# A hybrid encoder layer on one core: attention's products with v taken two steps at a time, sums of the down weights moved to gate/up, Silu, other tile sizes

## The chip, the cores and the metric

The kernel runs on one core of a Trainium2 chip. The core has TensorE (PE, whose weight loads are listed apart as PEld), VectorE (DVE), ScalarE (ACT), GpSimd (POOL) and SyncE (SP, which here only issues DMAs). The metric is the device time of one execution in microseconds (us), as the median of several executions. The kernel before took 1590.09 us as the median of three (1587.43 to 1590.85).

## What is computed

One layer on 1024 frames of 1024 features, in float32:

```python
h = rmsnorm(x, norm_mix_g)
z = h @ w_in
qa, fa, ia, ga, qb, kb, vb, gate_a, gate_b = jnp.split(z, split_at, axis=-1)
oa = hgrn2_mixer(qa, fa, ia, ga, ...)        # a gated recurrence, 4 heads of 128
ob = band_attention(qb, kb, vb, ...)         # 8 heads of 64, each chunk of 64 frames sees itself and 8 before
merged = sigmoid(gate_a) * (oa @ w_branch_a) + sigmoid(gate_b) * (ob @ w_branch_b)
x = x + merged @ w_out
h2 = rmsnorm(x, norm_ffn_g)
x = x + (silu(h2 @ w_ffn_gate) * (h2 @ w_ffn_up)) @ w_ffn_down      # 2816 inner features
h3 = rmsnorm(x, norm_ple_g)
x = x + sigmoid(h3 @ w_ple_gate) * (p @ w_ple_proj)
```

## The kernel before

Each large product keeps float32 accuracy by splitting both operands into a rounded part (`hi`) and a rest (`lo`): ACT copies the raw tile into `hi`, POOL or DVE subtracts to get `lo`, and PE adds three products, hi·hi, hi·lo and lo·hi (`gemm`, L137). Most matmuls have 128 rows, 128 columns of weights and 512 moving columns. Activations lie with features on partitions, so 1024 frames make two halves of 512.

The stages follow each other in `run` (L1861):

- **Recurrence.** `hgrn_in` (L311) makes the inputs of a head and `hgrn_mix` (L387) runs the recurrence of the head before; `weave` interleaves the two. The step `near` (L353) prepares the next head at the end of one.
- **Attention.** `attention` (L638) runs 32 steps, one for each pair of heads and each block of 128 frames. A step holds scores of two heads, transposes of q and k for the next step (`attn_stack`), transposes of the probabilities of the former step (`attn_pt`, inner name `pt`), products with v of the step before that (`attn_pv`, inner name `pv`) and, through `feed`, matmuls of later inputs. `pv(n)` has ten products of 128 x 128 by 64, two heads side by side in the two halves of the array's columns; a float32 product is two instructions. `pts` tiles have four buffers.
- **Gates, branches and the output product** (`gate_units`, `branches`, `out_proj`).
- **Gate/up.** `ff_pairs` (L1548) goes over 21 units after the first, which `second_part` does. An even unit makes 256 columns of the gate product, an odd one the same columns of the up product. `strassen` (L1461) computes a unit with seven products of 12 matmuls in three PSUM banks, where an eighth would be plain. The second product's bank is read into `u2` by DVE before the fourth product adds to it, and again into `u3` before the sixth adds to it. The stream `side` is advanced after each product: it makes the next unit's weights (`strassen_weights`, L1418), loads those of the unit after (`strassen_load`) and, in even units, forms sums of activations (`keep_acts`, L1519). `unit_gate` (L1404) finishes a gate product: DVE multiplies by the norm's row factor `rb`, ACT takes the sigmoid, POOL multiplies the two and then by `rb` once more.
- **Down, and the last product** (`ff_down`, `ple`).

The products of `out_proj`, `ff_down` and `ple` are also Strassen's, over quadrants a11, a21, a22, a12 of the weights; four sums of the quadrants (S1 to S4) are made in the kernel, stored to DRAM and read back as weights later. For `w_out` there are 4 such jobs, for `w_ffn_down` 11, each of four additions on 128 x 512. Before the change, 8 of the 15 jobs run on POOL during the recurrence, in halves of 256 columns (`quad_piece` and `quad_early`, L1083 to L1115, put beside the main stream by `beside`), and the other 7 on POOL in `gate_units` (`quad_slow`, L1047).

DVE, ACT and POOL work strictly in the order of the program where calls go through `self.V`, `self.A` and `self.G` (class `Pinned`), and so do PE and SP's queue. Because these helpers record the operation, most rows of a profile have L54 as their line; matmuls have L83, transposes L86, DMAs L78. In a row, `pm` is a PSUM tile, `s` a 128 x 1024 slot, `t` a 128 x 512 temporary (`stmp`), `q` a sum of weights, `wr` a raw weight, `whi`/`wlo` and `wh`/`wl` its split, `m` a small tile, `d` a DRAM tile. DMAs into SBUF wait until a tile's former content has been used.

Of the kernel before, what the change touches and what calls it, by code (L numbers as in the profile page):

```python
# [10 lines left out]
F32 = mybir.dt.float32  # L11
F32R = mybir.dt.float32r
U8 = mybir.dt.uint8
# [4 lines left out]
P = 128  # L18
# [15 lines left out]
PLAIN = 4  # L34
QUADS = 8

# [20 lines left out]
class Trunk:  # L57
# [175 lines left out]
    def setup(self):  # L233
        nc, d = self.nc, self.d
        cp = self.cp
        self.cols = cp.tile([P, N_COL], F32, name="cols")
        nc.scalar.dma_start(self.cols, d["cols"])
        self.eye = cp.tile([P, P], F32, name="eye")
        self.ones = cp.tile([P, 1], F32, name="ones")
        nc.vector.memset(self.ones, 1.0)  # L240
        self.onesr = cp.tile([P, P], F32R, name="onesr")
# [23 lines left out]
    def first_norm(self):  # L265
# [6 lines left out]
        for k in range(KC):  # L272
# [20 lines left out]
            if k == 3:  # L293
                self.load(self.eye, self.d["eye"])
                self.load(self.masks, self.d["masks"])
            if k:
# [341 lines left out]
    def attention(self):  # L638
# [40 lines left out]
        for n in range(whole + 2):  # L679
# [8 lines left out]
            if n < whole:  # L688
                scores(n, 1)
            drain(st)  # L690
            pt(n - 1, 1)
            next(feed, None)
            stage(n, 0)
            stage(n, 1)
            pv(n - 2)
            pt(n - 1, 0)
# [98 lines left out]
    def gate_units(self, sums):  # L795
# [42 lines left out]
        for n in range(units):  # L838

            def side():  # L840
                more = self.strassen_weights() if n + 1 < units else self.branch_first()
                if n == 0:
                    yield
                    yield
                next(more, None)
                if n + 2 < units:
                    self.strassen_load()
                yield
                for i, _ in enumerate(more):
                    for _ in range(1 + i % 2):  # L850
                        next(sums, None)
                    yield
# [229 lines left out]

    def quad_piece(self, src, k, sums, half):  # L1083

        G, cols = self.nc.gpsimd, HALF // 2
        w = self.slot(late=True)
        at = slice(half * cols, half * cols + cols)
        self.load(w[:, :].rearrange("p (i c) -> p i c", i=4), src.rearrange("p (i c) -> p i c", i=4)[:, :, at])
        for _ in range(5):
            yield  # L1090
        a11, a21, a22, a12 = [w[:, i * cols:i * cols + cols] for i in range(4)]
        for out, x, y, op in ((a22, a21, a22, ALU.add), (a21, a11, a21, ALU.subtract), (a11, a22, a11, ALU.subtract), (a12, a12, a11, ALU.subtract)):
            G.tensor_tensor(out, x, y, op)  # L1093
            yield
        yield
        to = slice(k % 2 * HALF + at.start, k % 2 * HALF + at.stop)
        for kind, part in zip(("S2", "S3", "S1", "S4"), (a11, a21, a22, a12)):
            if k % 2 == 0 and half == 0:
                sums[kind, k // 2] = self.spill()
            self.store(sums[kind, k // 2][:, to], part)  # L1100
        yield
        yield

    def quad_early(self, jobs):

        pieces = [self.quad_piece(*job, half) for job in jobs for half in range(2)]
        live = []
        while pieces or live:
            if pieces:
                live.append(pieces.pop(0))  # L1110
            for _ in range(6):
                for x in list(live):
                    if next(x, x) is x:
                        live.remove(x)
                yield  # L1115
# [288 lines left out]
    def unit_gate(self, c, half, ps):  # L1404
# [143 lines left out]
    def ff_pairs(self):  # L1548
        V, A, G = self.V, self.A, self.G

        units = len(self.sorder)
        self.acts = {}
        self.strassen_load()
        for n in range(1, units):
# [3 lines left out]
            def side():  # L1558
# [182 lines left out]
    def ple(self):  # L1741
# [32 lines left out]
        def after(kind, u, ps):  # L1774
# [35 lines left out]
        def side():  # L1810
# [30 lines left out]
            for i in range(4):  # L1841
                some(4)
                yield
            del todo[:]
# [16 lines left out]
    def run(self):  # L1861
# [18 lines left out]
        with ExitStack() as es:  # L1880
# [12 lines left out]
            with ExitStack() as mixer:  # L1893
                self.masks = mixer.enter_context(tc.tile_pool(name="levels", bufs=1)).tile([P, len(LEVELS), 64], U8, name="masks")
# [3 lines left out]
                jobs = [(d["oq"][k], k, self.osums) for k in range(4)] + [(d["wq"][k], k, self.sums) for k in range(NFF // 2)]  # L1898
                sums = self.quad_early(jobs[:QUADS])
                drain(beside(self.hgrn_in(0, outs), sums))  # L1900
                for h in range(3):
                    weave(beside(self.hgrn_in(h + 1), sums), self.hgrn_mix(h), 41500, 17000)
                self.feed = self.attn_in()
                weave(beside(chain(self.attn_v(), islice(self.feed, FIRST)), sums), self.hgrn_mix(3), 41500 + 1300 * FIRST, 17000)
                drain(sums)
# [52 lines left out]
def beside(main, side):  # L1958
    for x in main:
        next(side, None)  # L1960
        yield x

# [113 lines left out]
```

## Time and profile before

| | |
|---|---|
| median of three runs | 1590.09 us |
| the profiled execution, its own time | 1588.19 us |
| its span, first to last instruction | 1585.9 us |
| PE busy in the span | 1559.4 us |
| DVE busy | 1166.6 us |
| ACT busy | 639.8 us |
| POOL busy | 802.0 us |
| mean granted clock of PE | 0.996 |

The profile is one execution. A row of its timeline gives the start, the length, engine, line, operation, tiles (out<-in), shape and number of the merged instructions, and in brackets how long the engine was idle before and what released it. A row of its groups gives, behind the bar, busy us in all, mean ns of one, and the idle time before. PE's matmuls are pipelined, so two rows may overlap; the distance of their starts is what a matmul costs.

### The profile page before, as it was taken

How to read it: one execution, taken by the hardware profiler on the slowest of the kernel's cores; microseconds unless marked ns; L12 is line 12 of the kernel's file. 1: busy time of each engine (PE TensorE's matmuls, PEld its weight loads, DVE VectorE, ACT ScalarE, POOL GpSimd, SP SyncE). 2: the span in 40 equal slices, each digit the busy share in tenths (PEclk: the TensorE clock that was granted, in tenths of full speed). 3: DMA queues.
4: the chain of work that ended last, by engine and by line, in shares of the span. 5: the costliest groups of instructions: out<-in, count | busy, mean ns of one | idle time of the engine just before them, and what ended most of it. 6: DMA issues, size and time to landing. Idle time of an engine off the chain costs nothing.

```text
span 1585.9 us, 21744 instructions
## 1 busy us (share of the span) xinstructions
PE 1559.4 (98%) x8224; PEld 1311.1 (83%) x8224; DVE 1166.6 (74%) x1670; ACT 639.8 (40%) x1057; POOL 802.0 (51%) x461
## 2 busy tenths in 40 slices
PE   8999999999999999999999999999999999999997
PEld 6898888878888888888888888888888888888886
DVE  5656675468778778644898988888888856765658
ACT  6321211157777643421377322232222234445453
POOL 3764542123113059625330877777777754645454
PEclk9999999999999999999999999999999999999999
DMA  5443220220113358675244433333333278885344
GB/s 189 138 156 119 90 97 27 66 89 27 48 41 107 140 191 306 239 292 212 71 149 172 159 100 100 100 100 113 104 112 107 89 255 321 296 274 196 126 133 158
DMA packets 92649, 230.40 MB, mean 145 GB/s; under 512 B 9856, under 2 KB 26880, under 8 KB 92032
## 3 DMA queue, kind: packets, MB, share of 16 engines
q1 hardware_dynamic: 92400, 229.00, 42.1%
q8 instruction: 64, 1.05, 0.3%
q14 instruction: 41, 0.34, 0.1%
q10 hardware_dynamic: 144, 0.02, 0.0%
HBM read 163.70 MB, written 65.27 MB: 144 GB/s over the span
## 4 chain that ended last, share of the span: by engine, by line
PE 80%; DVE 6%; DMA 6%; POOL 4%; issue 2%; ACT 2%; SPq 1%; POOLq 0%; ACTq 0%; DVEq 0%
PE pm L83 77%; DVE s L54 3%; PE pm L86 3%; POOL wl L126 2%; DMA d<-s 1%; POOL s L1093 1%; DMA s<-in_oq 1%; DMA wr<-d 1%; DVE m L54 1%; SPq L78 1%; DMA wr<-in_qk 1%; DVE q L54 0%; POOL s L54 0%; ACT wh L123 0%; DMA wr<-in_fm 0%
## 5 line engine op out<-in xcount | busy, mean ns | idle before, releaser
L83 PE MATMUL pm<-s,wh 128*128 128x512 f32 (+1 forms) x1712 | 532.1, 392 | 6.6 <-ACT wh L123 5.2
L83 PE MATMUL pm<-s,whi 128*128 128x512 f32 x1568 | 483.0, 389 | 0.6 <-DVE t L54 0.6
L126 POOL TENSOR_TENSOR wl<-wr,wh 128x1024 fp32r<-128x1024 f32 (+2 forms) x108 | 269.5, 2500 | 321.1 <-ACT wh L123 314.9
L83 PEld LDWEIGHTS pm<-s,wh 128*128 128x128 f32 x1712 | 319.9, 189 | 73.5 <-ACT wh L123 5.6
L83 PEld LDWEIGHTS pm<-s,whi 128*128 128x128 f32 x1568 | 294.2, 188 | 61.9 <-DVE t L54 1.0
L83 PE MATMUL pm<-s,wl 128*128 128x512 f32 (+1 forms) x856 | 334.1, 390 | 0.3 <-POOL wl L126 0.3
L54 DVE TENSOR_TENSOR s<-s,s 128x512 f32<-128x512 f32 (+4 forms) x213 | 255.9, 1230 | 92.4 <-ACT s L54 58.3
L83 PE MATMUL pm<-s,wlo 128*128 128x512 f32 x784 | 305.2, 389 | 0.0
L83 PE MATMUL pm<-wh,s 128*128 128x256 f32 (+1 forms) x896 | 239.3, 341 | 0.0
L123 ACT CAST wh<-wr 128x1024 fp32r<-128x1024 f32 (+2 forms) x114 | 114.7, 1007 | 261.7 <-PE pm L83 132.8
L83 PEld LDWEIGHTS pm<-s,wl 128*128 128x128 f32 x856 | 161.3, 188 | 34.8 <-POOL wl L126 1.4
L83 PEld LDWEIGHTS pm<-s,wlo 128*128 128x128 f32 x784 | 147.2, 188 | 31.1 <-DVE wlo L54 0.5
L83 PEld LDWEIGHTS pm<-wh,s 128*128 128x128 f32 x896 | 155.4, 191 | 13.8
L83 PE MATMUL pm<-wl,s 128*128 128x256 f32 (+1 forms) x448 | 148.0, 330 | 0.4 <-POOL wl L126 0.4
L54 DVE TENSOR_TENSOR t<-pm,t 128x512 f32<-128x512 f32 x138 | 94.7, 686 | 71.4 <-PE pm L83 69.3
L54 POOL TENSOR_TENSOR wlo<-wr,whi 128x512 fp32r<-128x512 f32 (+1 forms) x53 | 109.9, 2083 | 72.2 <-ACT whi L54 72.2
L54 DVE TENSOR_TENSOR s<-pm,s 128x512 f32<-128x512 f32 (+1 forms) x134 | 87.3, 680 | 79.9 <-PE pm L83 78.7
L54 ACT CAST whi<-q 128x512 fp32r<-128x512 f32 (+1 forms) x81 | 61.5, 759 | 160.3 <-DVE q L54 140.5
L54 POOL TENSOR_TENSOR s<-s,t 128x512 f32<-128x512 f32 x44 | 76.6, 1741 | 81.7 <-ACT t L54 81.7
L54 ACT CAST s<-s 128x1024 fp32r<-128x1024 f32 (+1 forms) x94 | 90.2, 980 | 68.0 <-DVE s L54 33.7
L54 POOL TENSOR_TENSOR wlo<-q,whi 128x512 fp32r<-128x512 f32 x52 | 89.0, 1712 | 19.0 <-ACT whi L54 19.0
L83 PEld LDWEIGHTS pm<-wl,s 128*128 128x128 f32 x448 | 85.9, 192 | 5.9 <-POOL wl L126 0.6
(146 smaller groups left out, 1953.5 us busy)
## 6 DMA issues: line engine op xcount, KB each, us to landing
s<-d SPq DMA_DIRECT2D x67, 512.0 KB, 6.0
d<-s SPq DMA_DIRECT2D x115, 256.0 KB, 3.3
wr<-d SPq DMA_DIRECT2D x36, 512.0 KB, 3.7
s<-in_wq SPq DMA_DIRECT2D x22, 512.0 KB, 5.6
wr<-in_sg SPq DMA_DIRECT2D x22, 512.0 KB, 4.1
wr<-in_su SPq DMA_DIRECT2D x22, 512.0 KB, 4.1
s<-in_x SPq DMA_DIRECT2D x21, 512.0 KB, 7.8
d<-s SPq DMA_DIRECT2D x18, 512.0 KB, 4.9
```

The lines of the kernel that those rows point to most:

```text
L54: return lambda *a, **k: self.trunk.order(op(*a, **k), self.key)
L78: return self.order(self.nc.sync.dma_start(out, ap), "sp")
L83: return self.order(self.nc.tensor.matmul(*a, **k))
L86: return self.order(self.nc.tensor.transpose(*a, **k))
L123: self.nc.scalar.copy(hi[:, c], raw[:, c])
L126: rest.tensor_tensor(lo[:, c], raw[:, c], f32(hi[:, c]), ALU.subtract)
L1093: G.tensor_tensor(out, x, y, op)
```

## The change

- **Attention.** `pv` is no longer called once in every step between `stage(n, 1)` and `pt(n - 1, 0)`. In odd steps `pv(n - 3)` and `pv(n - 2)` are called one behind the other, after `drain(st)` and ahead of `pt(n - 1, 1)`.
- **Sums of weights.** `quad_early`, `quad_piece` and `beside` go. Five jobs run on POOL in `gate_units`, one addition at each call, and the other ten in `ff_pairs` on DVE, in 20 pieces of 256 columns (`quad_pieces`), which `side` advances from the second unit on. A piece has five steps: load, nothing, two additions, two additions, four stores. They have one buffer of their own (tag `quad`); the temporaries `tmp` fall from eight to seven.
- **Gate function.** ACT takes Silu in place of the sigmoid, and one of POOL's two multiplications goes.
- **Tiles.** `masks` is padded to 8 levels (512 bytes), `onesr` is allocated ahead of `ones`, `state` directly behind `rb`.
- **Down and last product.** The third weight of `ff_down` is asked for after two loads of activations. In `ple`, four additions go from POOL to DVE, and `m_split` is called once more at each of four points.

```diff
             drain(st)
+            if n % 2:
+                pv(n - 3)
+                pv(n - 2)
             pt(n - 1, 1)
             next(feed, None)
             stage(n, 0)
             stage(n, 1)
-            pv(n - 2)
             pt(n - 1, 0)
...
-                for i, _ in enumerate(more):
-                    for _ in range(1 + i % 2):
-                        next(sums, None)
+                for _ in more:
+                    next(sums, None)
                     yield
...
+    def quad_pieces(self, jobs):
+
+        V, cols = self.V, HALF // 2
+        for src, k, sums in jobs:
+            for half in range(2):
+                self.n += 1
+                w = self.fp.tile([P, 4 * cols], F32, tag="quad", name=f"qd{self.n}")
+                at = slice(half * cols, half * cols + cols)
+                self.load(w[:, :].rearrange("p (i c) -> p i c", i=4), src.rearrange("p (i c) -> p i c", i=4)[:, :, at])
+                yield
+                yield
+                a11, a21, a22, a12 = [w[:, i * cols:i * cols + cols] for i in range(4)]
+                V.tensor_tensor(a22, a21, a22, ALU.add)
+                V.tensor_tensor(a21, a11, a21, ALU.subtract)
+                yield
+                V.tensor_tensor(a11, a22, a11, ALU.subtract)
+                V.tensor_tensor(a12, a12, a11, ALU.subtract)
+                yield
+                for kind, part in zip(("S2", "S3", "S1", "S4"), (a11, a21, a22, a12)):
+                    if k % 2 == 0 and half == 0:
+                        sums[kind, k // 2] = self.spill()
+                    self.store(sums[kind, k // 2][:, k % 2 * HALF + at.start:k % 2 * HALF + at.stop], part)
+                yield
...
-        A.activation(s, g[:, hs], AF.Sigmoid)
-        G.tensor_tensor(g[:, hs], g[:, hs], s, ALU.mult)
-        G.tensor_tensor(g[:, hs], g[:, hs], self.rb[:, hs], ALU.mult)
+        A.activation(s, g[:, hs], AF.Silu)
+        G.tensor_tensor(g[:, hs], s, self.rb[:, hs], ALU.mult)
...
+        pieces = self.quad_pieces(self.later)
...
                 for _ in more:
                     next(keep, None)
+                    if n > 1:
+                        next(pieces, None)
                     yield
                 drain(keep)
+                if n % 4 == 0:
+                    next(pieces, None)
+                if n == units - 2:
+                    drain(pieces)
...
-        self.weights(0, ahead=3)
+        self.weights(0, ahead=2)
         yield
         for _ in range(2):
             self.down_load()
             yield
+        self.weights(0, ahead=3)
...
-                todo.append(out(2 * u + 1, h0, u3[u]))
+                todo.append(out(2 * u + 1, h0, u3[u], V))
...
                 some(4)
+                self.m_split()
                 yield
...
-                sums = self.quad_early(jobs[:QUADS])
-                drain(beside(self.hgrn_in(0, outs), sums))
+                drain(self.hgrn_in(0, outs))
...
-                drain(self.gate_units(self.quad_slow(jobs[QUADS:])))
+                drain(self.gate_units(self.quad_slow(jobs[:QUADS])))
+                self.later = jobs[QUADS:]
...
-SMALL = {"rb": 1, "rtok": 1, "epsv": 1, "state": 1, "t8": 2, "t4": 4, "mx2": 4, "den": 4}
+SMALL = {"rb": 1, "state": 1, "rtok": 1, "epsv": 1, "t8": 2, "t4": 4, "mx2": 4, "den": 4}
...
-FFN = {"q1024": 1, "q512": 3, "raw": 2, "tmp": 8}
+FFN = {"q1024": 1, "q512": 3, "raw": 2, "tmp": 7, "quad": 1}
```

More of the change, by code (lines that the diff above doesn't have):

```diff
@@ L34 @@
 PLAIN = 4
-QUADS = 8
+QUADS = 5
 C_MIX, C_FFN, C_PLE, C_ON, C_GQ, C_GK, C_LB = 0, 8, 16, 24, 25, 26, 27
@@ L238, in setup @@
         self.eye = cp.tile([P, P], F32, name="eye")
+        self.onesr = cp.tile([P, P], F32R, name="onesr")
         self.ones = cp.tile([P, 1], F32, name="ones")
         nc.vector.memset(self.ones, 1.0)
-        self.onesr = cp.tile([P, P], F32R, name="onesr")
         nc.vector.tensor_copy(self.onesr, self.ones[:, :].to_broadcast([P, P]))
@@ L294, in first_norm @@
                 self.load(self.eye, self.d["eye"])
-                self.load(self.masks, self.d["masks"])
+                self.load(self.masks[:, :len(LEVELS), :], self.d["masks"])
             if k:
@@ L1081, in quad_slow @@
         store(*prev)
[L1083 to L1114, printed above, removed]
+    def quad_pieces(self, jobs):
[19 more added lines that the diff above has]
+                    self.store(sums[kind, k // 2][:, k % 2 * HALF + at.start:k % 2 * HALF + at.stop], part)
@@ L1893, in run @@
             with ExitStack() as mixer:
-                self.masks = mixer.enter_context(tc.tile_pool(name="levels", bufs=1)).tile([P, len(LEVELS), 64], U8, name="masks")
+                self.masks = mixer.enter_context(tc.tile_pool(name="levels", bufs=1)).tile([P, 8, 64], U8, name="masks")
                 outs = self.first_norm()
@@ L1897, in run @@
                 self.late = mixer.enter_context(tc.tile_pool(name="late1", bufs=2))
-                jobs = [(d["oq"][k], k, self.osums) for k in range(4)] + [(d["wq"][k], k, self.sums) for k in range(NFF // 2)]
-                sums = self.quad_early(jobs[:QUADS])
-                drain(beside(self.hgrn_in(0, outs), sums))
+                drain(self.hgrn_in(0, outs))
                 for h in range(3):
-                    weave(beside(self.hgrn_in(h + 1), sums), self.hgrn_mix(h), 41500, 17000)
+                    weave(self.hgrn_in(h + 1), self.hgrn_mix(h), 41500, 17000)
                 self.feed = self.attn_in()
-                weave(beside(chain(self.attn_v(), islice(self.feed, FIRST)), sums), self.hgrn_mix(3), 41500 + 1300 * FIRST, 17000)
-                drain(sums)
+                weave(chain(self.attn_v(), islice(self.feed, FIRST)), self.hgrn_mix(3), 41500 + 1300 * FIRST, 17000)
                 self.attn_setup()
@@ L1910, in run @@
                 self.fp = Small(tc, xs, FFN, "gates_", reuse_waits="tile")
-                drain(self.gate_units(self.quad_slow(jobs[QUADS:])))
+                jobs = [(d["oq"][k], k, self.osums) for k in range(4)] + [(d["wq"][k], k, self.sums) for k in range(NFF // 2)]
+                drain(self.gate_units(self.quad_slow(jobs[:QUADS])))
+                self.later = jobs[QUADS:]
             with ExitStack() as xs:
@@ L1955, in drain @@
             return e.value
[L1958 to L1961, printed above, removed]
 def weave(main, side, main_ns, side_ns):
```

## The prediction

> **What bounds the kernel now.** I read the head of the page first, then the stretches of single stages, then the rows of TensorE (PE) and of its feeders in the stages that the change touches.
>
> ```profile
> span 1585.9 us, 21744 instructions
> PE 1559.4 (98%) x8224; PEld 1311.1 (83%) x8224; DVE 1166.6 (74%) x1670; ACT 639.8 (40%) x1057; POOL 802.0 (51%) x461
> ```
>
> PE is busy 98% of the span: an edit can win only where PE itself does less, or where it stands still (26.5 us in all). An edit that loads another engine costs nothing until PE waits for it.
>
> ```profile
> 160.00:180.00 20.00, 17.45 (x139) 16.98 (x137) 14.05 (x24) 4.83 (x11) 13.75 (x12) 0.91 0.26 83
> 220.00:240.00 20.00, 18.46 (x172) 17.03 (x172) 17.96 (x28) 6.03 (x12) 10.87 (x9) 1.00 0.22 76
> 280.00:300.00 20.00, 20.00 (x137) 16.48 (x136) 9.64 (x26) 0.36 (x1) 0.00 (x0) 1.00 0.01 2
> 500.00:520.00 20.00, 20.00 (x158) 17.11 (x157) 14.80 (x52) 13.47 (x31) 0.23 (x1) 1.00 0.38 133
> 580.00:600.00 20.00, 20.00 (x90) 16.55 (x89) 17.10 (x17) 6.67 (x11) 18.35 (x12) 1.00 0.92 303
> 895.00:1255.00 360.00, 360.00 (x1590) 298.20 (x1589) 319.27 (x295) 102.31 (x150) 270.75 (x152) 1.00 0.31 101
> ```
>
> Columns: the stretch, its length, busy us and instructions of PE, PEld, DVE, ACT and POOL, the granted clock, the DMA share, GB/s. In the recurrence (160 to 240) PE loses time where POOL works beside DVE; without POOL work (280 to 300) it loses none. In attention (500 to 520) PE is full. In gate/up (895 to 1255) PE is full too, but VectorE (DVE) works 319.27 of 360 us beside a POOL at 75%: this stage has the least room, and the change puts work into it.
>
> **Attention.** The change takes no product away; it joins the products of two steps, so the array goes to half-width (128*64) matmuls and back 16 times rather than 32.
>
> ```profile
> 498.77 0.71 PE L83 MATMUL pm<-s,wh 128*128 128x512 f32 x2
> 499.55 0.62 PE L83 MATMUL pm<-s,wh 128*128 128x512 f32 x2
> 500.01 0.40 PE L83 MATMUL pm<-s,wl 128*128 128x512 f32 x1
> 500.34 1.31 PE L83 MATMUL pm<-m,s 128*64 128x128 f32 x20
> 501.37 0.28 PE L83 MATMUL pm<-m,s 128*64 128x128 f32 x2
> 501.58 0.77 PE L86 MATMUL pm<-eye,m 128*128 128x128 f32 x5
> 502.11 0.71 PE L83 MATMUL pm<-s,wh 128*128 128x512 f32 x2
> 505.19 0.71 PE L86 MATMUL pm<-eye,m 128*128 128x128 f32 x5
> 505.65 0.71 PE L83 MATMUL pm<-s,wh 128*128 128x512 f32 x2
> ```
>
> Starts tell the price. Gate matmuls follow each other every 0.23 us (500.01 less 499.55, two of them), but the first half-width one comes 0.33 after the last: 0.10 lost. Its ten pairs start every 0.11 (1.03 us over nine), the transposes come 0.21 after the last pair: 0.10 lost. Five transposes then take 0.53 instead of 0.46 (505.19 to 505.65): 0.07. One round trip is 0.27 us, 16 of them 4.3 us. Against it stands that a step without products lasts 6.9 (498.77 to 505.65) less 1.5 (500.24 to 501.58 and the slower transposes), 5.4 us, while DVE has about 14.80/20 x 6.9 = 5.1 us of work in it, so PE can wait a little for the next step's scores; the 2.5 us of products in the other step stand ahead of the transposes and give the time back. Nothing queues behind these matmuls but PE's own stream. Bounds: 4.3 gained; nothing gained where each short step waits 0.27. I take **-3.8**.
>
> **Sums taken out of the recurrence.** 8 of the 15 jobs were there: 16 loads, 64 POOL ops and 64 stores.
>
> ```profile
> L1093 POOL TENSOR_TENSOR s<-s 128x256 f32<-128x256 f32 x64 | 55.8, 873 | 52.4 <-DMA s<-in_wq 24.4 <-DMA s<-in_oq 21.4 <-DMA d<-s 2.9
> 158.49 2.60 DVE L323 TENSOR_SCALAR s<-s,lb,lb 128x512 f32<-128x512 f32 x1
> 150.24 0.55 DVE L323 TENSOR_SCALAR s<-s,lb,lb 128x512 f32<-128x512 f32 x1 [0.70 <-ACT s L322]
> 173.26 0.81 PE L83 MATMUL pm<-s,s 128*128 128x128 f32 x4 [1.76 <-ACT s L447]
> ```
>
> The same DVE instruction takes 0.55 us alone and 2.60 beside POOL; a few of these push the end of a head late, and PE stands 1.76 us. The two stretches lose 2.55 and 1.54 us, and the clock of 0.91 in the first is another 1.8 (9% of 20). Bounds: all 5.9, or nothing if the heads' own work suffices for the wait. The stretch at 280, PE full and POOL empty, is nearer the first: **-5**. The 55.8 us on POOL and the DMAs themselves are beside PE and count nothing.
>
> The jobs left in the gate stage fall from 7 to 5 (28 POOL ops to 20). POOL is at 18.35 of 20 there, but PE at 20.00: nothing to win.
>
> **Gate/up: Silu and the ten moved jobs.** Two units, one gate and one up, take 360/1590 x 168 = 38.0 us of PE (168 matmuls), so the stretch holds 9.46 such pairs; DVE is idle 40.7/9.46 = 4.3 us in each.
>
> ```profile
> L54 POOL TENSOR_TENSOR s<-s,t 128x512 f32<-128x512 f32 x37 | 65.8, 1780 | 70.1 <-ACT t L54 70.1
> L54 DVE TENSOR_TENSOR q<-wr,q 128x512 f32<-128x512 f32 x19 | 43.7, 2300 | 0.0
> L54 DVE TENSOR_TENSOR s<-t,s 128x512 f32<-128x512 f32 x30 | 40.2, 1342 | 2.4
> L54 DVE TENSOR_TENSOR q<-wr,wr 128x512 f32<-128x512 f32 x19 | 33.8, 1781 | 0.0
> L54 DVE TENSOR_TENSOR q<-q,wr 128x512 f32<-128x512 f32 x19 | 31.6, 1664 | 0.7
> L54 DVE TENSOR_TENSOR s<-t,rb 128x512 f32<-128x512 f32 x27 | 23.0, 854 | 0.9
> L54 DVE TENSOR_TENSOR q<-wr 128x512 f32<-128x512 f32 x19 | 17.4, 917 | 0.0
> L54 DVE TENSOR_TENSOR s<-s,s 128x512 f32<-128x512 f32 x10 | 6.8, 678 | 0.0
> L54 DVE TENSOR_TENSOR s<-s 128x512 f32<-128x512 f32 x9 | 6.2, 684 | 0.0
> 1102.53 1.21 DVE L54 TENSOR_TENSOR wlo<-q,whi 128x1024 fp32r<-128x1024 f32 x1
> 1121.69 2.31 DVE L54 TENSOR_TENSOR wlo<-q,whi 128x1024 fp32r<-128x1024 f32 x1
> 1124.29 1.42 DVE L54 TENSOR_TENSOR t<-pm,t 128x512 f32<-128x512 f32 x2 [0.29 <-PE pm L83]
> 1111.56 2.85 POOL L54 TENSOR_TENSOR wlo<-wr,whi 128x1024 fp32r<-128x1024 f32 x1
> ```
>
> Silu takes out the POOL multiplication of the first row. POOL falls from 270.75 to 205 us of the 360, from 75% to 57%. DVE ops on 512 columns in SBUF take 0.68 us at best; the eight DVE rows above at 128x512 hold 152 ops in 202.7 us, 1.33 each, so each waits 0.65 us, and at 57% of POOL 0.50 (0.65 x 57/75). A pair has 16 of them: **2.4 us of DVE freed per pair** (with the 1024-column ones some 2.8).
>
> The moved jobs bring 20 pieces, one per unit over 19 units: 20 loads, 80 stores and 80 DVE ops of 128x256, 8 per pair. Alone, one costs 0.41 us (0.68 less half of 1.21 - 0.68), 0.33 where it follows another op as these do. The wait is the question. A lone 512 op grows from 0.68 to 1.78 beside POOL and a 1024 op from 1.21 to 2.31: 1.10 more in both, so the wait belongs to the POOL op in its way, not to the DVE op's size, and a small op waits as long as a large one. So 0.33 + 0.50 = 0.83 each, 6.6 per pair, and 3.8 more on DVE after Silu's relief. Of the 4.3 us idle I take half as fillable: the pieces stand at fixed places in an in-order queue, and idle time that lies before them, waiting for a product, isn't theirs. That leaves 3.8 - 2.15 = 1.65 us per pair, 9.5 pairs: **+15.7**. What is late next: behind the pieces on DVE stand the sums that read a bank (u2 after the second product, u3 after the fourth) before PE may add the next product to it. The row at 1124.29 shows 0.29 us of slack there, and one product later (12 x 0.227 = 2.7 us, less the op's 0.68) PE stops. Bounds: below nothing is excluded, as PE is already full here; nothing, if all idle time is fillable, up to 3.8 x 9.5 = 36, if none is.
>
> The Trainium skill (SBUF — State Buffer, section "SBUF: two separate sides") speaks against the pieces: the port pair that DVE and GpSimd share is an exclusive lock held for a whole instruction, and the loser blocks fully. The 1.10 us at both sizes agrees. By that rule the sum is the +15.7 above; by a proportional split a half-size op would wait 0.25, 8 x 0.58 less 2.8 is 1.8 per pair, which the idle time hides, and the term would be nothing.
>
> ```profile
> d<-s SPq DMA_DIRECT2D x115, 256.0 KB, 3.3
> s<-in_wq SPq DMA_DIRECT2D x22, 512.0 KB, 5.6
> 538.08 1.28 ACT L54 ACT_TABLE_LOAD   x1
> ```
>
> On SP's queue a piece's load waits for the former piece's stores, and the weight load of the unit after next stands behind it: 3.3 + 5.6 us of a 19 us unit, with DMA at 0.31. No charge; if that cover went, each wait would be up to 3.3 us. A second function costs one or two table loads of 1.28 us more on ACT, idle 258 of 360 us: no charge, 2.6 at most.
>
> **The end.**
>
> ```profile
> 1575.35 0.28 PE L83 MATMUL pm<-s,wl 128*128 128x256 f32 x1
> 1563.98 5.82 DVE L54 TENSOR_TENSOR s<-s,s 128x1024 fp32r<-128x1024 f32 x5 [1.64 <-ACT s L54]
> 1565.89 6.32 POOL L54 TENSOR_TENSOR s<-s,s 128x512 f32<-128x512 f32 x4 [5.90 <-DVE s L54]
> ```
>
> PE ends 10 us before the span does; DVE's queue sets the end. Four additions go from POOL (6.32) to DVE: 2.4 us more, but the five ops at 1563.98 shrink about as much with POOL gone. One split (1.21, as at 1102.53) moves ahead into a stage before. **-1**, between 0 and -4. Aligned tiles and one temporary fewer I take at nothing: PE is full in the rows at 500, 580 and 895, where these tiles are in use, and an eighth temporary covers a buffer that is read a product (2.7 us) before its next use; a wait there would be one op, 0.68. The third down weight is asked for two loads later, behind two whose products cover it; without them it would cost one landing, 3.3 us.
>
> **Sum.** -3.8 - 5 + 15.7 - 1 = +5.9 us on the profiled execution's 1588.19; that one lies 1.90 under the median of the runs, 1590.09, on whose scale I forecast **1596.0**.
>
> **Rivals.** *Gate/up hides the pieces* (faster): Silu's relief and the idle time cover them. It decides at 4.3 + 2.8 = 7.1 us per pair, 0.89 per piece op, if all idle time is fillable; my 0.83 is under that. For it, no DVE wait of PE in 360 us; against it, the 0.29. Time 1590.1 - 9.8 = 1580.3. *No idle time is fillable*: +36 in place of 15.7, 1616. *The joined products win nothing*, since each short step waits for DVE: 1599.8. *The recurrence keeps its stalls*, as its own splits on POOL hold DVE up: 1601.0.
>
> **Numbers.** Forecast 0.42, hidden pieces 0.28, none fillable 0.10, joining without effect 0.10, stalls kept 0.10. About 0.2%, 3.2 us, is what a measurement of this kernel can tell from no change: under 1586.9 is faster, over 1593.3 slower. Faster takes the first rival and 0.02 of the forecast's low side; no change 0.12; slower the rest, 0.58. The range 1579 to 1612 takes in the first rival and most of the fourth term's bounds; the forecast's own is 1587 to 1606.
>
> **What would show it.** Half-width runs of 40 in attention, 16 of them, with PE's stage some 4 us shorter; no PE wait on ACT L447 near 173 and a clock of 1.00 there; in gate/up, PE waits on DVE t before the fourth or sixth product, with 128x256 DVE ops of 0.4 to 1.6 us. Forecast and sum are wrong if PE stays full from 895 to 1255, or if these ops stay near 0.4.

## The result and the profile after

The changed kernel takes 1605.91 us, the median of six runs (1602.1 to 1607.43), against 1589.93 for the kernel before on the same chip: ratio 1.0094, 95% interval 1.0069 to 1.0119. By that ratio it is slower by about 15 us (the medians differ by 16.0); 5.9 was forecast. The profiled execution takes 1605.46 us, 17.3 more than that of before.

Head of the page of the kernel after:

```profile
span 1603.7 us, 21710 instructions
PE 1558.6 (97%) x8224; PEld 1313.0 (82%) x8224; DVE 1163.0 (73%) x1754; ACT 638.2 (40%) x1059; POOL 652.3 (41%) x341
```

PE executes as many instructions as before and is busy as long, but in a span longer by 17.8 us. POOL lost 150 us of work, and DVE is no busier (1163.0 against 1166.6) although it has 84 additions more (80 of the pieces, four moved in the last product). So the time is not work: it is PE standing still.

To see where, I took the same matmul at five borders of stages: the last products of the recurrence, of attention, the 16 transposes before gate/up, the first matmul of the down stage, and PE's last. Timeline of the kernel before (start, length, engine, line, operation, tiles), then of the kernel after:

```profile
321.60 0.49 PE L83 MATMUL pm<-state,s 128*128 128x128 f32 x2 [0.96 <-DVE state L54]
...
531.83 0.73 PE L83 MATMUL pm<-s,wh 128*128 128x512 f32 x2
...
873.79 1.95 PE L83 MATMUL pm<-eye,m 128*128 128x128 f32 x16
...
1284.50 0.61 PE L83 MATMUL pm<-s,wh 128*128 128x512 f32 x2
```

```profile
313.79 0.49 PE L83 MATMUL pm<-state,s 128*128 128x128 f32 x2
...
522.22 0.61 PE L83 MATMUL pm<-s,wh 128*128 128x512 f32 x2
...
862.45 1.95 PE L83 MATMUL pm<-eye,m 128*128 128x128 f32 x16
...
1302.26 0.62 PE L83 MATMUL pm<-s,wh 128*128 128x512 f32 x2
...
1592.42 0.28 PE L83 MATMUL pm<-s,wl 128*128 128x256 f32 x1
```

| stretch | before, us | after, us | change | forecast |
|---|---|---|---|---|
| recurrence, to 321.60 / 313.79 | 321.60 | 313.79 | -7.8 | -5 |
| attention | 210.23 | 208.43 | -1.8 | -3.8 |
| from there to the transposes | 341.96 | 340.23 | -1.7 | 0 |
| gate/up | 410.71 | 439.81 | +29.1 | +15.7 |
| down and last product | 290.85 | 290.16 | -0.7 | 0 |
| after PE's last matmul began | 10.55 | 11.28 | +0.7 | -1 |
| sum | 1585.9 | 1603.7 | +17.8 | +5.9 |

Gate/up decides. The stretches of the kernel after that answer to those of before (stretch, length, busy us and instructions of PE, PEld, DVE, ACT and POOL, granted clock, DMA share, GB/s):

```profile
160.00:180.00 20.00, 19.80 (x168) 19.60 (x167) 12.40 (x26) 5.02 (x11) 5.55 (x4) 1.00 0.00 1
220.00:240.00 20.00, 19.27 (x167) 18.79 (x167) 13.61 (x27) 4.81 (x11) 5.07 (x4) 1.00 0.08 28
492.00:512.00 20.00, 20.00 (x172) 17.80 (x172) 13.60 (x47) 12.71 (x30) 0.00 (x0) 1.00 0.37 131
890.00:1274.00 384.00, 367.77 (x1583) 300.31 (x1582) 323.85 (x368) 100.27 (x149) 198.97 (x112) 0.98 0.44 148
```

In the recurrence PE is now nearly full and its clock 1.00. In gate/up PE stands for 16 of 384 us and the clock is 0.98, while DVE, on which it waits, is idle for 60.15 us. An engine that is idle 16% of a stage and makes another wait is not short of time; it is busy at the wrong moment. The view of the waits in gate/up, and around the longest one the timeline of DVE, POOL and PE:

```profile
PE pm L83 <- DVE t L54: 20.1, 13, 3.0
```

```profile
1041.70 2.96 DVE L54 TENSOR_TENSOR qd<-qd 128x256 f32<-128x256 f32 x2
1044.59 3.42 DVE L54 TENSOR_TENSOR wlo<-q,whi 128x1024 fp32r<-128x1024 f32 x1
1047.93 1.94 DVE L54 TENSOR_TENSOR qd<-qd 128x256 f32<-128x256 f32 x2
1049.78 1.41 DVE L54 TENSOR_TENSOR t<-pm,t 128x512 f32<-128x512 f32 x2
...
1042.91 4.01 POOL L54 TENSOR_TENSOR wlo<-wr,whi 128x512 fp32r<-128x512 f32 x2
1046.89 2.24 POOL L54 TENSOR_TENSOR wlo<-q,whi 128x512 fp32r<-128x512 f32 x1
...
1047.12 0.39 PE L83 MATMUL pm<-s,wlo 128*128 128x512 f32 x1
1050.52 1.22 PE L83 MATMUL pm<-s,whi 128*128 128x512 f32 x2 [3.01 <-DVE t L54]
1051.54 0.63 PE L83 MATMUL pm<-s,wlo 128*128 128x512 f32 x1
1051.97 1.05 PE L83 MATMUL pm<-s,whi 128*128 128x512 f32 x2
```

In DVE's queue stand two additions of a piece, a split, two more additions, and only then comes `t<-pm,t`, the read of the bank (u3) for which the sixth product waits. All three run beside POOL's splits, and take 2.96, 3.42 and 1.94 us; two such additions take 0.88 us where nothing is in their way (row 932.24 further down), the split 1.21 (row 1102.53 of the prediction). PE stands 3.01 us, and its next matmuls start every 0.43 us (1051.97 less 1051.54) instead of every 0.227: half speed, for some 5 us. (POOL's row of 4.01 us holds two splits, one of 512 and one of 1024 columns; the view merges them under the first one's shape.)

### The profile page after: what moved, and what is told of

Its sections match the earlier page's. It is cut to its first block, busy times and chain, and to the rows that moved or that the text cites. A ratio compares the mean times of both kernels' runs of the same rounds, so it can differ in the third digit from the quotient of the medians.

```text
span 1603.7 us, 21710 instructions
## 1 busy us (share of the span) xinstructions
PE 1558.6 (97%) x8224; PEld 1313.0 (82%) x8224; DVE 1163.0 (73%) x1754; ACT 638.2 (40%) x1059; POOL 652.3 (41%) x341
## 5 line engine op out<-in xcount | busy, mean ns | idle before, releaser
L83 PE MATMUL pm<-s,whi 128*128 128x512 f32 x1568 | 489.1, 393 | 20.1 <-DVE t L54 20.1
L54 DVE TENSOR_TENSOR s<-s,s 128x512 f32<-128x512 f32 (+4 forms) x217 | 263.5, 1244 | 82.3 <-ACT s L54 44.7
L54 POOL TENSOR_TENSOR wlo<-wr,whi 128x512 fp32r<-128x512 f32 (+1 forms) x53 | 116.2, 2200 | 95.0 <-ACT whi L54 95.0
L54 POOL TENSOR_TENSOR s<-t,rb 128x512 f32<-128x512 f32 x44 | 70.3, 1601 | 115.4 <-ACT t L54 115.4
L54 POOL TENSOR_TENSOR wlo<-q,whi 128x512 fp32r<-128x512 f32 x52 | 83.5, 1606 | 79.5 <-ACT whi L54 73.2
L54 ACT ACTIVATE t<-s 128x512 f32<-128x512 f32 x44 | 27.8, 633 | 167.2 <-DVE s L54 164.3
```

The costliest lines, as they stand in the source:

```text
L54: return lambda *a, **k: self.trunk.order(op(*a, **k), self.key)
L83: return self.order(self.nc.tensor.matmul(*a, **k))
```

## The experiments

Each run was timed beside the kernel before, whose median was 1587.7 to 1590.4 us on the chips that were used, so runs are compared by their ratios. "Stretch" is the time from attention's border to the first down matmul (752.67 us before: gate/up with the stage ahead of it, taken together because a short wait near 866 us is followed by slow matmuls in some executions and not in others). The last column is what PE waited for DVE t in gate/up.

| run | median, us | ratio to before, 95% interval | stretch, us | waits, us (times) |
|---|---|---|---|---|
| before | 1590.09 | | 752.67 | 0.6 (1) |
| after | 1605.91 | 1.0094 (1.0069 to 1.0119) | 780.04 | 20.1 (13) |
| sums_back | 1590.0 | 1.0002 (0.999 to 1.0015) | 756.8 | 3.0 (1) |
| no_additions | 1579.91 | 0.9937 (0.9919 to 0.9955) | 756.37 | 3.0 (1) |
| fixed_phase | 1590.97 | 1.0009 (0.9999 to 1.002) | 765.23 | 9.9 (11) |
| table_early | 1604.46 | 1.0095 (1.007 to 1.0121) | 775.67 | 17.1 (12) |
| placed | 1578.9 | 0.9941 (0.9927 to 0.9956) | 754.17 | 2.1 (1) |
| narrow | 1616.76 | 1.0189 (1.0175 to 1.0204) | 791.35 | 27.7 (13) |
| pairs_only | 1587.79 | 1.0003 (0.9993 to 1.0014) | 755.46 | 0.6 (1) |
| silu_only | 1588.07 | 1.0002 (0.9991 to 1.0013) | 752.91 | 0 |
| placed_temp | 1578.01 | 0.9924 (0.9911 to 0.9936) | 754.08 | 2.1 (1) |
| sums_back8 | 1589.39 | 0.9993 (0.9978 to 1.0008) | 753.21 | 0 |
| placed_sigmoid | 1599.57 | 1.006 (1.0045 to 1.0076) | 772.62 | 14.2 (11) |

**Is it the pieces, and which part of them?** Two runs. sums_back is the changed kernel with `quad_early` in the recurrence again:

```diff
-QUADS = 5
+QUADS = 8
...
-                drain(self.hgrn_in(0, outs))
+                sums = self.quad_early(jobs[:QUADS])
+                drain(beside(self.hgrn_in(0, outs), sums))
...
-                    if n > 1:
-                        next(pieces, None)
```

> The changed kernel with its sums of weights put back where they were (8 jobs on POOL in the recurrence, 7 in the gate stage, none in gate/up); attention, Silu, tiles and the end stay changed. If the pieces are what gate/up lost its 29 us by, all but the first wait of 3.2 us goes there (26 less), and the recurrence gives its 8 us back: about 1587.5. If the recurrence gained by the aligned tiles and not by the sums taken out, it keeps its gain: about 1579.5. If Silu or the tiles are to blame for gate/up, the waits on DVE t stay there and the time is over 1600.

no_additions keeps the pieces' DMAs and leaves out their additions:

```diff
-                V.tensor_tensor(a22, a21, a22, ALU.add)
-                V.tensor_tensor(a21, a11, a21, ALU.subtract)
                 yield
-                V.tensor_tensor(a11, a22, a11, ALU.subtract)
-                V.tensor_tensor(a12, a12, a11, ALU.subtract)
```

> The changed kernel whose pieces in gate/up are loaded and stored but not added (the 80 DVE additions are left out, so ten of the fifteen sums are the bare quadrants). If the additions in DVE's queue make PE wait, gate/up is full but for the first wait: about 1605.5 - 26 = 1579.5. If the 20 loads and 80 stores on SP's queue make weights late, the time stays within 3 us of 1605.

Measured 1590.0 and 1579.91. Without the additions PE is full from 890 us on, with all 100 DMAs still there:

```profile
890.00:1259.00 369.00, 369.00 (x1628) 305.43 (x1628) 291.03 (x302) 102.78 (x153) 211.37 (x114) 1.00 0.47 156
```

So SP's queue is not the cause, and the 80 additions on DVE are: they make 23.7 of the 27.4 us that the stretch grew by. The other 3.7 stand in no_additions as well (4.1 in sums_back): there PE makes the first wait, 3.0 us, and slow matmuls follow it. With the sums back, the last products of the recurrence begin 8.8 us later than in the kernel after, although the aligned tiles stay: the recurrence gained by the sums, not by the tiles. In all traces with sums in the recurrence they begin at 320.5 to 324.9 us, in all others at 313.8 to 314.6.

**Is it how much, or where?** fixed_phase begins the pieces one unit earlier and takes out the extra steps:

```diff
-                    if n > 1:
-                        next(pieces, None)
+                    next(pieces, None)
...
-                if n % 4 == 0:
-                    next(pieces, None)
```

> The changed kernel with the pieces begun one unit earlier (20 units times 5 steps) and without the extra step in every fourth unit, so that the additions always stand behind the fourth and the fifth product of a unit. Theory of room (DVE's work in a pair is more than its idle time, as the prediction summed it): the same 80 additions against the same work, 1605 within 3. Theory of place (DVE has idle time enough, 60 of 384 us in the changed kernel, and PE waits only where additions stand ahead of u2 or u3): the waits of 1.3 to 3.2 us before a sixth product go, some 1.0 us before the fourth product of each odd unit stays as in the first units (about 10 us in all), and so does the first 3.2: about 1590.

placed puts the same 80 additions elsewhere, and one dummy Silu early:

```diff
-                for _ in more:
+                if n == 1:
+                    next(pieces)
+                for i, _ in enumerate(more):
                     next(keep, None)
-                    if n > 1:
+                    if i - (3 if n % 2 else 1) in (0, 1):
                         next(pieces, None)
...
+        A.activation(self.warm, self.ones, AF.Silu)
```

In it a call makes all four additions of a piece, and the next call stores them and loads the next piece.

> The changed kernel with the same 20 pieces in other places of DVE's queue and with the early dummy Silu: in even units all four additions of a piece stand behind the third product (between u2 and u3, where the run without additions leaves DVE idle for 2 us and POOL has nothing to do), in odd units behind the fifth. Theory of room (the 80 additions cost what the prediction summed, wherever they stand): gate/up still loses about 16 us, 1595. Theory of place: gate/up is full from 890 on, PE waits for DVE t less than 3 us in all, and the time is about 1579.

Measured 1590.97 and 1578.9, where place foretold 1590 and 1579, and room 1605 and 1595. The groups of the additions (busy us, mean ns of one) of the kernel after, of fixed_phase and of placed, in this order, and then gate/up's stretch in placed:

```profile
L54 DVE TENSOR_TENSOR qd<-qd 128x256 f32<-128x256 f32 x76 | 67.2, 884 | 1.3
```

```profile
L54 DVE TENSOR_TENSOR qd<-qd 128x256 f32<-128x256 f32 x76 | 70.3, 924 | 1.3
```

```profile
L54 DVE TENSOR_TENSOR qd<-qd 128x256 f32<-128x256 f32 x80 | 36.6, 457 | 2.1
```

```profile
890.00:1255.00 365.00, 365.00 (x1612) 302.24 (x1611) 322.19 (x378) 102.57 (x152) 209.06 (x114) 1.00 0.49 157
```

In fixed_phase an addition costs more than in the kernel after, 0.924 against 0.884 us, and yet PE waits half as long (1.6 us of the difference is the first wait, which is 1.40 there). So the place counts by itself, whatever an addition costs. In placed both change: the same additions cost 0.457, and 70 of the 80 take 0.42, as POOL has no instruction beside them there. The dummy Silu is a small part of the gain: table_early, further down, has it without the places and is 1.5 us under the kernel after. In placed DVE is busy 322.19 of 365 us, 88%, more than the 84% of the kernel after, and PE misses nothing.

**Does the wait belong to the op or to its size?** narrow cuts each addition in two:

```diff
-                V.tensor_tensor(a22, a21, a22, ALU.add)
+                for b11, b21, b22, b12 in cuts:
+                    V.tensor_tensor(b22, b21, b22, ALU.add)
```

> The changed kernel with each addition of a piece cut into two of 128x128 (160 instead of 80, same columns in all, same places). If a DVE op waits out the POOL op in its way whatever its own size, each half waits as long as a whole one (0.88 us measured less some 0.38 of own work, 0.5): about 0.7 to 0.75 each, 55 us in the stage become some 110 (76 ops were in 67.2 us), and PE waits for 20 us more at least: over 1625. If the wait is a share of the op's own length, the halves wait half as long, the group stays near 70 us and the time within 6 of 1605.

Measured 1616.76, between the two. The group of its additions, then some of them from its timeline (four of 128x128 in a row), and last some from the timeline of the kernel after (two of 128x256):

```profile
L54 DVE TENSOR_TENSOR qd<-qd 128x128 f32<-128x128 f32 x152 | 91.2, 660 | 0.0
```

```profile
909.08 4.19 DVE L54 TENSOR_TENSOR qd<-qd 128x128 f32<-128x128 f32 x4
...
914.93 3.08 DVE L54 TENSOR_TENSOR qd<-qd 128x128 f32<-128x128 f32 x4
...
931.17 1.97 DVE L54 TENSOR_TENSOR qd<-qd 128x128 f32<-128x128 f32 x4
...
933.67 0.88 DVE L54 TENSOR_TENSOR qd<-qd 128x128 f32<-128x128 f32 x4
```

```profile
913.65 2.94 DVE L54 TENSOR_TENSOR qd<-qd 128x256 f32<-128x256 f32 x2
...
929.76 1.96 DVE L54 TENSOR_TENSOR qd<-qd 128x256 f32<-128x256 f32 x2
...
932.24 0.88 DVE L54 TENSOR_TENSOR qd<-qd 128x256 f32<-128x256 f32 x2
...
964.93 4.04 DVE L54 TENSOR_TENSOR qd<-qd 128x256 f32<-128x256 f32 x2
```

A row takes 0.88 us, or that and one, two or three portions of 1.03 to 1.10 us more, with ops of either size. What a portion is shows beside POOL. First an addition of the kernel after with the POOL instruction in its way, then another one with its own:

```profile
929.76 1.50 DVE L54 TENSOR_TENSOR qd<-qd 128x256 f32<-128x256 f32 x1
929.25 1.73 POOL L54 TENSOR_TENSOR wlo<-q,whi 128x512 fp32r<-128x512 f32 x1
...
966.48 2.49 DVE L54 TENSOR_TENSOR qd<-qd 128x256 f32<-128x256 f32 x1
966.13 2.56 POOL L54 TENSOR_TENSOR wlo<-wr,whi 128x1024 fp32r<-128x1024 f32 x1
```

All 34 waiting additions of the kernel after end 0.28 to 0.29 us behind the end of the POOL instruction in their way, and the 47 of narrow, half as large, 0.15 us behind it: what varies is how long POOL has still to go. Behind 512 columns of POOL an addition loses up to 1.1 us, behind 1024 columns 2.1 to 2.2, which is what looks like two portions; of the 80 additions 29 met the one kind, 5 the other, and 46 neither. In narrow it was 36, 11 and 113 of 160, with the same losses. So the wait belongs to the POOL instruction in the way, as the prediction read it from the ops of 512 and 1024 columns; neither theory had said that several small ops in a row may meet one POOL instruction and pay for it once. Twice as many ops paid 1.36 times as much (91.2 over 67.2), not 2 and not 1. The Trainium skill (SBUF — State Buffer, section "SBUF: two separate sides") calls the shared port pair an exclusive lock that is held for a whole instruction; waits that go by the length of the POOL instruction and not by the size of the waiting op agree with it, and a split of bandwidth does not.

**The parts alone.** pairs_only is the kernel before with the products joined:

```diff
+            if n % 2:
+                pv(n - 3)
+                pv(n - 2)
             pt(n - 1, 1)
...
-            pv(n - 2)
```

> The kernel before with the products with v joined and nothing else. By the prediction's price (16 round trips of 0.27 us) attention's stage, 210.0 us from its first to its last gate matmul in the kernel before, falls to 206.2 and the time by 3.8. By the trace of the changed kernel (seams 3.7 less, new waits of PE on DVE m some 2 more) the stage is 208.2 and the time falls by 1.8. If the joining wins nothing, 210.

silu_only is the kernel before with Silu:

```diff
-        A.activation(s, g[:, hs], AF.Sigmoid)
-        G.tensor_tensor(g[:, hs], g[:, hs], s, ALU.mult)
-        G.tensor_tensor(g[:, hs], g[:, hs], self.rb[:, hs], ALU.mult)
+        A.activation(s, g[:, hs], AF.Silu)
+        G.tensor_tensor(g[:, hs], s, self.rb[:, hs], ALU.mult)
```

> The kernel before with Silu and one POOL multiplication in place of the sigmoid and two, nothing else. By the prediction Silu frees DVE (2.8 us of a pair) but PE was full, and its table loads cost nothing: no change, with DVE's busy time from 895 to 1255 falling from 319 to about 293. By the first wait that the changed kernel and the one with the sums put back both show, the table load makes PE wait 3.2 us before the fourth product of the first unit, and slow matmuls follow: 5 us slower than before.

Neither can be told from the kernel before by its time (1587.79 and 1588.07 beside 1587.68). In pairs_only attention takes 208.4 us between the borders of the table above, 1.8 less than the 210.2 before, as in the kernel after; a gain of 1.8 us lies within the interval of its time. The waits of PE in attention there:

```profile
PE pm L86 <- DVE m L54: 2.3, 4, 1.3
PE pm L83 <- DVE m L54: 1.0, 2, 0.7
```

The kernel before waited 1.0 us for DVE m in this stage. silu_only frees DVE and wins nothing, as PE was full: DVE falls from 319.27 to 284.39 us in the same stretch.

```profile
895.00:1255.00 360.00, 360.00 (x1590) 298.10 (x1589) 284.39 (x294) 100.90 (x149) 210.10 (x113) 1.00 0.30 101
```

The second expectation for silu_only, 5 us slower by its table load, was wrong; the next runs say why.

**The first wait of gate/up.** The kernel after loses 3.03 us before the fourth product of the first unit, ahead of any addition. ACT's timeline in the kernel after, and in silu_only:

```profile
867.68 1.28 ACT L54 ACT_TABLE_LOAD   x1 [2.66 <-DMA d<-t]
```

```profile
875.97 1.28 ACT L54 ACT_TABLE_LOAD   x1
```

With seven temporaries ACT first waits for a store out of a temporary, and the table load for Silu comes behind that; with eight it comes at once. table_early adds a dummy Silu and, in the down stage, a dummy sigmoid; placed_temp lends placed an eighth temporary for the first part of gate/up; sums_back8 gives sums_back eight. Of the lines below the first belongs to table_early and the placed runs, the second to table_early, the block with `extra` to placed_temp, and the last two lines to sums_back8:

```diff
+        A.activation(self.warm, self.ones, AF.Silu)
...
+        self.A.activation(self.warm, self.ones, AF.Sigmoid)
...
+                with tc.tile_pool(name="extra", bufs=1, reuse_waits="tile") as extra:
+                    self.extra.append(extra.tile([P, HALF], F32, tag="extra", name="extra"))
+                    self.second_part()
...
-FFN = {"q1024": 1, "q512": 3, "raw": 2, "tmp": 7, "quad": 1}
+FFN = {"q1024": 1, "q512": 3, "raw": 2, "tmp": 8}
```

> The changed kernel with one dummy Silu on a 128x1 tile in the first part of the gate/up stage and one dummy sigmoid in the down stage, so that the two table loads of 1.28 us happen where ACT has time. If the table load before the first Silu makes the split of the next weights late, the first wait of gate/up falls from 3.2 to about 0.8 us and the last ones after PE's end by up to 1.2: about 3 us faster than the changed kernel, 1602. If the load is hidden as the prediction had it, no change, 1605.

> The run with the placed pieces and one more 128x512 temporary for the first part of gate/up alone (its room is given to the pieces' buffer after that). If ACT's wait of 1.0 to 2.6 us on a store of a temporary (DMA d<-t), which stands in every trace with seven temporaries and in none with eight, is what makes the first u2 late, that wait and the first one of PE (2.1 us) go, slow matmuls behind them too: 2 us faster than the placed run, about 1576.8. If the table load or the work itself makes it late, it stays at 1579.

> The run with the sums put back, with eight temporaries instead of seven; its sums are not in gate/up, so the place of the pieces' buffer is free for it. If the seventh temporary makes the first wait of gate/up (3.15 us with slow matmuls behind it), that falls to under 0.8 us and PE's time between the transition and the second unit by some 3 us. If it is the table load of Silu, the wait stays at 3 us.

In table_early the first wait is gone from the trace (12 waits instead of 13, the stretch 4.4 us shorter); its median is only 1.5 us under that of the kernel after, and the two ratios cannot be told apart. In sums_back8 the wait is gone too (0.5 us for another tile, wlo, is left), and its stretch is 3.6 us shorter than in sums_back. In placed_temp ACT no longer waits for the store, but PE still waits 2.1 us: that expectation failed. In table_early, silu_only and sums_back8 slow matmuls near 860 to 870 us make PE come later; in placed and placed_temp PE comes 1.6 us earlier and waits for the same DVE work. fixed_phase and narrow have the store wait, the late load and the slow matmuls, and wait 1.40. So load and store wait behind each other lengthen the wait by some 1 us (3.0 against 2.1 without slow matmuls, 1.40 against 0 to 0.6 with them). The store wait alone costs nothing, as placed, which has it, and placed_temp, which has not, both wait 2.1 us; nor does the load alone, in silu_only and sums_back8. The rest stands in placed_temp, which has neither; whether it is a lack of DVE time in the first unit is not shown. What share of the median this is stays open.

**Is Silu needed?** placed_sigmoid is the changed kernel with placed additions and the gate function of before:

```diff
-        A.activation(s, g[:, hs], AF.Silu)
-        G.tensor_tensor(g[:, hs], s, self.rb[:, hs], ALU.mult)
+        A.activation(s, g[:, hs], AF.Sigmoid)
+        G.tensor_tensor(g[:, hs], g[:, hs], s, ALU.mult)
+        G.tensor_tensor(g[:, hs], g[:, hs], self.rb[:, hs], ALU.mult)
```

> The changed kernel with the placed pieces, but with the sigmoid and POOL's two multiplications as before. If the pieces need the DVE time that Silu frees (35.0 us of DVE work in a pair of units before, 4 of it freed, and 8 additions of 0.46 us in 38.1), the sum is 38.7 at least, DVE falls behind, and PE loses 1 us or more in each of ten pairs: over 1588. If the place alone decides, the time is about 1579.

```profile
890.00:1270.00 380.00, 366.04 (x1591) 296.94 (x1590) 373.36 (x373) 100.81 (x149) 267.74 (x150) 1.00 0.46 149
```

The group of its additions:

```profile
L54 DVE TENSOR_TENSOR qd<-qd 128x256 f32<-128x256 f32 x80 | 79.0, 987 | 2.1
```

Measured 1599.57. Here DVE is busy 373.36 of 380 us, and PE loses 14. This is what a lack of room looks like. But the expectation had put 0.46 us for an addition, and it is 0.987: with POOL's second multiplication back, 40 of the 80 meet a POOL instruction again. So Silu does two things that this run does not part: it frees DVE, and it empties POOL beside the places where the additions stand.

## Why the prediction was right in sign and short in size

- **What bounds gate/up, and where it stalls: right.** PE waits on DVE t before the fourth and the sixth product, 13 times; the additions lie between 0.41 and 2.61 us, with a mean of 0.884 where 0.83 was put (0.42 of own work and 0.46 of wait for 0.33 and 0.50).
- **"Of the 4.3 us idle I take half as fillable": the step that failed.** Silu freed 34.9 us over 9.46 pairs (319.27 less 284.39), 3.7 per pair instead of 2.8; the pieces took 8 times 0.884, 7.1 per pair. By the sum DVE gains 3.4 us of work in 4.3 us of idle time: with all of it fillable the term would have been nothing. Gate/up grew by 29.1 us all the same, and the stretch by 27.4; with other places for the same ops it grew by 12.6 (fixed_phase, where an addition cost more) or 1.5 (placed, where it cost half). How much idle time can be filled is not a share, it follows from where the ops stand against the two reads of a bank, and the shifting phase of `n % 4` carried the additions through good and bad places alike. The +15.7 had the right sign because half was a guess between two ends, and the true one hangs on the place. The time of 1605.91 lies at the upper end of the forecast's own range, 1587 to 1606; that it lies inside is in part luck, as the recurrence gave back 2.8 us more than was put.
- **What the sum left out.** The waits make 20.1 of the 29.1 us, and 3.0 of that is the first wait, which is not the additions'. Of the other 9, some 5.5 are 27 matmuls at half speed behind three of the 13 waits; the rest is about 0.3 us at each wait, by which the matmuls next to it start later than the wait alone would have it. No row of the kernel before tied slow matmuls to a wait in this stage, but the 0.91 that I charged in the recurrence was such a row (the clock is 0.66 from 173 to 178 us, behind the wait of 1.76).
- **The recurrence, -5: right in kind, -7.8.** The long wait on ACT L447 is gone and the clock is 1.00; the traces with and without the sums, above, bear it out. I bounded the gain by two stretches of 20 us; the other heads lost time as well (the kernel after is 2.6 us ahead by 146 us).
- **Attention, -3.8: the seams are as priced, the waits were not.** Sixteen runs of half-width matmuls instead of 32 save 3.7 us, summed over the starts at their borders; but PE now waits 3.3 us for DVE m instead of 1.0, in six places. My reason for neglecting this, that the long steps give the time back, did not hold. Timeline of the kernel after, one joined run and one such wait in the step behind it:

```profile
479.88 2.40 PE L83 MATMUL pm<-m,s 128*64 128x128 f32 x40
...
489.62 0.44 PE L86 MATMUL pm<-eye,m 128*128 128x128 f32 x2 [1.35 <-DVE m L54]
```

- **The end, -1: no change.** 10.55 and 11.28 us, and 10.4 to 11.4 in the other runs: the same chain of DVE ops stands behind the last matmul. The later third weight costs nothing (-0.7 in the down stage).
- **Table loads and the eighth temporary, each taken at nothing: right alone, wrong together**, by some 1 us and the slow matmuls behind.
- **The rival of the hidden pieces**, 1580.3, did not come in this kernel, whose additions cost 0.884, just under its limit of 0.89; placed is that rival, at 1578.9.

placed_temp beats both kernels: 0.9924 of the time before (0.9911 to 0.9936), about 12 us. It can't be told from placed, at 0.9941 (0.9927 to 0.9956).

## What to carry to other kernels

Idle time of an in-order engine is worth something only at the places where it lies: before moving work there, fold the engine's idle time by its position in the repeating unit, mark which of its ops the bottleneck waits for, and put the new ops behind those. Put DVE ops on two SBUF tiles where POOL is idle; there they cost half (0.457 against 0.884 us here). An edit that merely frees an engine (Silu here) earns nothing until something fills the room, so judge the two together. A mean can hide two kinds: of the 80 additions 46 take 0.42 us and the other 34 some 1.6.

## What the runs showed of the hardware that was not expected

- DVE's wait for POOL goes by the POOL instruction in the way: up to 1.1 us behind 512 columns, 2.1 to 2.2 behind 1024, for additions of 128 and of 256 columns alike, and several small ops in a row can pass behind one wait. `t<-pm,t`, which reads one of its operands from PSUM, doesn't wait: all 93 in gate/up of the kernel after take 0.68 to 0.69 us, 44 of them beside a POOL instruction.
- Slow matmuls (427 ns from start to start instead of 227) follow much shorter waits than I had thought, and not always. The wait of 0.3 us on DVE m near 866 us stands in the kernel before and after (there near 857); behind it the clock fell in the one and not in the other:

```profile
866.00:870.00 4.00, 3.74 (x12) 3.01 (x12) 3.57 (x4) 3.31 (x5) 2.56 (x1) 0.58 0.34 131
```

```profile
856.00:862.00 6.00, 5.74 (x29) 4.77 (x29) 5.44 (x7) 5.34 (x9) 2.56 (x1) 1.00 0.30 105
```

Ahead of this wait stand 16 matmuls of one moving column, 1.84 us in the kernel before, so the wait need not be the whole reason. The 3.03 us wait at 883.78 in the kernel after was followed by full speed, the 3.01 us one at 1050.52 by half. The Trainium skill (TensorE: Matmul & The Clock Gate, section "Part 1: The HAM clock gate (the "warmup" mystery)") has the clock fall to half behind an idle window of about 3.4 us; the waits in gate/up of the kernel after are all shorter, and the longest there of all runs, 3.67 us at 1058.40 in narrow, was followed by full speed.

The clock's records in the traces narrow down what decides. In each of the 13 traces every fall of the clock and every return lies on a grid of steps of 3.41 us, placed differently in each trace, and the clock stays low for one step or two, but for the fall behind PE's last matmul. In the kernel after, the step ahead of the fall at 1049.71, the low stretch itself, and the step that holds most of the 3.03 us wait:

```profile
1046.30:1049.71 3.41, 1.21 (x6) 0.67 (x4) 3.38 (x3) 0.00 (x0) 2.82 (x2) 1.00 0.00 0
1049.71:1056.53 6.82, 6.01 (x14) 4.75 (x15) 3.22 (x6) 0.00 (x0) 0.00 (x0) 0.50 0.56 200
879.06:882.47 3.41, 1.69 (x8) 1.07 (x6) 3.38 (x3) 2.14 (x4) 3.41 (x3) 1.00 0.46 154
```

In gate/up of all traces the clock fell behind each step in which PE was busy for up to 1.31 us, and behind none with 1.62 or more; in between, at 1.51 to 1.58, both happened. (In the recurrence it also fell behind one step with 1.65.) A grid point cuts narrow's wait of 3.67 us into steps with 1.51 and 1.64 us of work. So it matters where a wait lies on the grid, and not only how long it is. The falls near 860 to 870 don't fit this count, since the matmuls of one column count as busy there; what decides them is open.
